# Two layers of a hybrid backbone: a recurrence's ScalarE steps are merged over two parts, emitted in smaller pieces behind the attention's exponentials, and the values' projection moves to other memory

## The chip, the cores and the metric

One core of one Trainium2 chip. The metric is the device time of one execution in microseconds; the median of three runs of the kernel before is 3753.56 us (3748.58 to 3754.28). Engines: TensorE (PE; its weight loads PEld), VectorE (DVE), ScalarE (ACT), GpSimd (POOL) and SyncE (SP), which here only issues transfers.

## The reference

Two post-norm layers over 1024 latent and 256 context tokens of width 1024, all in float32. Layer 0 mixes with an 8-head attention and, beside it, an S5 recurrence; layer 1 with a gated linear recurrence; each layer ends with a convolutional feed-forward part. The change concerns layer 0's mixer:

```python
q_l, k_l, v_l = _mla_qkv(cq_l, ckv_l, kr_l, q_norm, w_uq, kv_norm, w_ukv, rope)
att_l = _blocked_attend(q_l, k_all, v_all)          # softmax(q k^T * scale) v, 8 heads
ys_c, fin_c = _s5_bidirectional(us_c, disc, c_re, c_im, None, need_ctx)
ys_l, _ = _s5_bidirectional(us_l, disc, c_re, c_im, fin_c, True)   # complex diagonal scan
z = jax.nn.gelu(y + d_g * us); out = z * jax.nn.sigmoid(z @ w_glu)
y_lat = jnp.concatenate([att_l, out], -1) @ w_out
```

The recurrence's state is complex: each state has a real and an imaginary part, and a step multiplies it by a complex number that is constant per state, s += a * s_before, that is (re, im) += (ar*re - ai*im, ai*re + ar*im).

## The kernel before

`body` runs setup, the first modulation, loading of x, `s5_setup` (the recurrence's matrices), `in_proj` (the combined input projection), `attention`, `mix_out0` (gate and output projection) and then the feed-forward parts and layer 1, which the change does not edit. float32 matrices are split in a high part that TensorE reads in one pass and a low remainder (`split`: ScalarE copies the high part, VectorE or GpSimd subtracts), and a product is three matmuls (`mm3`, lines 103 to 105).

`attention` first projects the values of all heads (`pv`, pool `vp`), scales them on ScalarE (`vo`) and stores them in DRAM (`vd`). Then it interleaves generators; each `yield` ends a step, and `merge` takes from the generator with most of its steps left. `qk(h)` loads head h's weights, projects keys (`pk`) and queries (`pq`), finds the largest score of a row (`pS` at line 797, reduced on VectorE) and puts it in row 96 of `QT`. `attend(h)` takes 22 tiles of 128 keys: scores `pS`, exponential `p` on ScalarE, its split `ph`/`pl`, and three matmuls into `po`; three block results go out as `ao`. `A1` brings the modulation of later stages (`pada`, 80 steps with 512 KB each). `S5Half.run` is the recurrence (`S`), in two halves of 16 groups: `pV` (input matmuls, evicted into `H`), two levels of an up-sweep, 38 sequential steps on GpSimd, two levels of a down-sweep, then `pY` (output matmuls), the gelu `z`, and a store to `Zd`, which `mix_out0` loads again as `z`.

A level (`bulk`) multiplies a part of `H` by a constant per partition and state on ScalarE into `bt` (one activation per state q, part in, part out) and adds it to `H` on VectorE (direction 0) or GpSimd (direction 1). PSUM has eight banks, given by letters in `BANKS`: in the attention A has two for scores, B one for `po`, C three for `qk`, D one for the recurrence, E one for the modulation. `behind(k, inst)` keeps what is issued within it behind `inst`; `k.pace` is the last score matmul. A scheduler of the framework then sets each engine's order: emission gives the priority, buffers and readiness by its own estimates the rest; on the chip each engine, and SyncE's queue of transfers, goes strictly in that order. Pools are stacks at the left or right end of the memory, and a tile waits for what was in its place. Before, `vp` lies on the left, where the pool `W` of `qk` follows it; the exponentials' pool `PP` is on the right.

Of the kernel before, what the change touches and what calls it, by code (L numbers as in the profile page):

```python
# [17 lines left out]
D = 1024  # L18
# [28 lines left out]
def constants():  # L47

    ident = np.eye(128, dtype=np.float32)
    d16 = (np.arange(128)[:, None] % 16 == np.arange(16)[None, :]).astype(np.float32)  # L50
    pos = np.arange(SEQ)
    inv = (10000.0 ** (-np.arange(8, dtype=np.float32) / np.float32(8))).astype(np.float32)
    ar = (pos // 64).astype(np.float32)[:, None] * inv
    ac = (pos % 64).astype(np.float32)[:, None] * inv
    ang = np.concatenate([ar, ar, ac, ac], -1).T
    rope = np.zeros((64, T), np.float32)
    rope[:32, :SEQ] = np.cos(ang)
    rope[32:, :SEQ] = np.sin(ang)
    rope[:32, SEQ:] = 1.0
    s = np.arange(128)  # L60
    masks = np.zeros((128, 7, 128), np.int32)
    for l in range(7):
        h = 1 << l
        masks[:, l] = ((s[:, None] // (2 * h) == s[None] // (2 * h)) & (s[:, None] // h != s[None] // h))
    return {"k_ident": ident, "k_d16": d16, "k_rope": rope, "k_mask": masks.reshape(128, 896),
            "k_sel": np.repeat(np.eye(8, dtype=np.float32), 64, 1)}
# [152 lines left out]
def lower_bounds(k, A, S):  # L219
# [18 lines left out]
    k.mask = k.const([128, 7, 128], mybir.dt.uint8, tag="mask")  # L238

# [367 lines left out]
def in_proj(k, A, wp, places):  # L607
# [67 lines left out]
    for i in range(0, 896, 448):  # L675
        m32 = sp([128, 448], I32, tag="sq", bufs=2)
        nc.sync.dma_start(out=m32[:], in_=A["k_mask"][:, i:i + 448])
        nc.gpsimd.tensor_copy(k.mask[:].rearrange("p l t -> p (l t)")[:, i:i + 448], m32[:])
# [15 lines left out]
def attention(k, A):  # L694
# [22 lines left out]
    vp = Pool(k, "vp")  # L717
# [96 lines left out]
    def attend(h):  # L814
        b = h % 2
        q, kk_, v = QT[b], KT[b], Vt[b]
        for s, e in BLK:
# [3 lines left out]
            for i, t in enumerate(tiles):  # L821
# [3 lines left out]
                nc.scalar.activation(p[:, :n], ps[:, :n], AF.Exp, scale=SCALE)  # L825
# [20 lines left out]
    for _ in zip_longest(qk(0), some(8, A1)):  # L846
        pass
    for h in range(8):
        merge((24, attend(h)), *([(20, qk(h + 1))] if h < 7 else []), *([(34, some(34, S)), (12, some(12, A1))]))
# [10 lines left out]
class S5Half:  # L860
# [11 lines left out]
    def run(self):  # L872
        k, nc, P = self.k, self.k.nc, self.P
        E = nc.gpsimd
        for hh in range(2):
# [10 lines left out]
            for p in range(8):  # L886
# [11 lines left out]
                yield 1  # L898
# [3 lines left out]
            def bulk(i, up, d):  # L902
# [5 lines left out]
                src, dst = ((h, 2 * h), (h, 0))[d] if up else ((0, h), (2 * h, h))[d]  # L908
                for q0 in range(0, 8, m):
# [3 lines left out]
                    for b in range(2):  # L913
                        for a in range(2):
                            for q in range(m):
                                nc.scalar.activation(t[b][:, a, q], raw(H, 16 * 161 * d + (8 * b + q0 + q) * 161 + src, [[2 * h, n]]),  # L916
                                                     AF.Copy, scale=Mh[:, i, d, a, b, q0 + q:q0 + q + 1])
                        o = raw(H, 16 * 161 * d + q0 * 161 + dst, [[8 * 161, 2], [161, m], [2 * h, n]])
                        if b == 0:
                            yield 1  # L920
                    for b in range(2):
                        e.tensor_tensor(o, o, t[b], op=OP.add)
                    yield 1

            def both(levels, up):

                g = [chain(*(bulk(i, up, d) for i in levels)) for d in range(2)]
                for x in zip_longest(*g):
                    yield 1
# [7 lines left out]
            for (pf, cf, df), (pb, cb) in zip(seq, seb):  # L937
# [7 lines left out]
                yield 1  # L945
            yield from both((1, 0), False)
            for p in range(8):
# [8 lines left out]
                for q in range(2):  # L956
# [8 lines left out]
                    nc.scalar.activation(t[:, q], ps[:, :160], AF.Square, scale=0.5)  # L965

# [7 lines left out]
                yield 1  # L974
# [571 lines left out]
def body(tc, A, out, stop=None, taps=None):  # L1546
    nc = tc.nc
    k = Ctx()
    k.tc, k.nc, k.pace = tc, nc, None
# [128 lines left out]
```

## Time and profile before

| | |
|---|---|
| median of 3 runs | 3753.56 us |
| profiled execution | 3752.72 us |
| its span | 3750.9 us |
| mean granted TensorE clock | 0.967 of 2.4 GHz |
| TensorE busy | 3562.0 us, 95% |
| VectorE, ScalarE, GpSimd busy | 54%, 32%, 29% |
| first to last exponential | 333.5 to 903.5 us |

An average over 3.75 ms says little on one stage: ScalarE's 32% are up to 19 of 20 us in some stretches of the attention. Matmuls are pipelined, and a recorded one is longer than the time to the next one's start, so a busy TensorE may still have small gaps.

### The profile page before, as it was taken

How to read it: one execution, taken by the hardware profiler on the slowest of the kernel's cores; microseconds unless marked ns; L12 is line 12 of the kernel's file. 1: busy time of each engine (PE TensorE's matmuls, PEld its weight loads, DVE VectorE, ACT ScalarE, POOL GpSimd, SP SyncE). 2: the span in 40 equal slices, each digit the busy share in tenths (PEclk: the TensorE clock that was granted, in tenths of full speed). 3: DMA queues.
4: the chain of work that ended last, by engine and by line, in shares of the span. 5: the costliest groups of instructions: out<-in, count | busy, mean ns of one | idle time of the engine just before them, and what ended most of it. 6: DMA issues, size and time to landing. Idle time of an engine off the chain costs nothing.

```text
span 3750.9 us, 47623 instructions
## 1 busy us (share of the span) xinstructions
PE 3562.0 (95%) x19001; PEld 2899.7 (77%) x19001; DVE 2008.3 (54%) x3201; ACT 1210.6 (32%) x2312; POOL 1086.1 (29%) x1041
## 2 busy tenths in 40 slices
PE   6987899889999999999998999999999999999997
PEld 3764565556788888888887889898987888888885
DVE  7735654556464444444447555565664744444445
ACT  2236756666342111111124322222231411212123
POOL 3626523723351111111124311211122622222122
PEclk8997999889999999999999999999999999999998
DMA  7463354314111111111110210111122111111111
GB/s 246 120 163 98 95 139 139 99 38 147 53 33 42 40 38 36 34 40 34 34 46 29 74 34 29 34 32 37 32 67 89 51 40 51 51 40 55 41 46 45
DMA packets 294303, 243.06 MB, mean 65 GB/s; under 512 B 41214, under 2 KB 255576, under 8 KB 293056
## 3 DMA queue, kind: packets, MB, share of 16 engines
q1 hardware_dynamic: 289152, 227.32, 20.4%
q10 hardware_dynamic: 4928, 12.69, 1.0%
q8 instruction: 149, 2.44, 0.3%
q14 instruction: 74, 0.61, 0.1%
HBM read 203.79 MB, written 38.28 MB: 65 GB/s over the span
## 4 chain that ended last, share of the span: by engine, by line
PE 82%; ACT 4%; DVE 3%; POOL 3%; DMA 2%; issue 1%; SPq 0%; ACTq 0%; POOLq 0%; DVEq 0%
PE pa L105 5%; PE pa L103 5%; PE pa L104 5%; PE po L103 5%; PE pg L103 5%; PE pg L105 5%; PE pg L104 5%; PE po L104 5%; PE po L105 5%; PE ph L104 3%; PE ph L105 3%; PE ph L103 3%; PE pA L1429 3%; ACT bt L916 3%; PE pmix L103 2%; PE pmix L104 2%
## 5 line engine op out<-in xcount | busy, mean ns | idle before, releaser
L114 POOL TENSOR_TENSOR w<-ws,w 128x1024 fp32r<-128x1024 f32 (+1 forms) x205 | 499.9, 2443 | 1575.0 <-ACT w L111 1464.8
L1061 DVE SCALAR_TENSOR_TENSOR acc<-po,mod,acc 128x512 f32<-128x512 f32 (+1 forms) x456 | 309.4, 679 | 557.2 <-PE po L105 556.9
L103 PE MATMUL po<-hh,w 128*128 128x512 f32 (+1 forms) x912 | 341.6, 375 | 11.0 <-DVE acc L1061 9.2
L111 ACT ACTIVATE w<-ws 128x1024 fp32r<-128x1024 f32 (+1 forms) x207 | 216.9, 1049 | 408.7 <-PE pg L105 165.4
L104 PE MATMUL po<-hl,w 128*128 128x512 f32 (+1 forms) x912 | 335.4, 368 | 5.9 <-DVE hl L114 5.8
L105 PE MATMUL po<-hh,w 128*128 128x512 f32 (+1 forms) x912 | 334.8, 367 | 0.0
L103 PE MATMUL pa<-uh,w 128*128 128x512 f32 (+1 forms) x896 | 331.6, 370 | 0.9 <-ACT w L111 0.8
L104 PE MATMUL pa<-ul,w 128*128 128x512 f32 (+1 forms) x896 | 330.1, 369 | 0.1
L105 PE MATMUL pa<-uh,w 128*128 128x512 f32 (+1 forms) x896 | 326.4, 370 | 0.8 <-POOL w L114 0.8
L103 PE MATMUL pg<-uh,w 128*128 128x512 f32 (+1 forms) x872 | 324.2, 372 | 1.9 <-ACT w L111 1.9
L104 PE MATMUL pg<-ul,w 128*128 128x512 f32 (+1 forms) x872 | 322.6, 370 | 0.0
L105 PE MATMUL pg<-uh,w 128*128 128x512 f32 (+1 forms) x872 | 321.5, 372 | 0.6 <-POOL w L114 0.6
L103 PE MATMUL ph<-uh,w 128*128 128x512 f32 (+1 forms) x624 | 239.8, 385 | 1.2 <-ACT uh L1047 1.2
L104 PE MATMUL ph<-ul,w 128*128 128x512 f32 (+1 forms) x624 | 235.6, 378 | 0.8 <-DVE ul L1049 0.8
L105 PE MATMUL ph<-uh,w 128*128 128x512 f32 (+1 forms) x624 | 235.5, 377 | 0.0
L103 PEld LDWEIGHTS po<-hh,w 128*128 128x128 f32 x912 | 172.9, 190 | 46.1 <-DVE acc L1061 12.0
L104 PEld LDWEIGHTS po<-hl,w 128*128 128x128 f32 x912 | 173.6, 190 | 37.9 <-DVE hl L114 7.0
L1114 ACT ACTIVATE a<-pa 128x512 f32<-128x512 f32 (+1 forms) x112 | 61.3, 547 | 431.6 <-PE pa L105 430.5
L105 PEld LDWEIGHTS po<-hh,w 128*128 128x128 f32 x912 | 173.5, 190 | 30.2
L103 PEld LDWEIGHTS pa<-uh,w 128*128 128x128 f32 x896 | 168.7, 188 | 32.7 <-ACT w L111 1.0
L105 PEld LDWEIGHTS pa<-uh,w 128*128 128x128 f32 x896 | 168.6, 188 | 32.2 <-POOL w L114 1.3
L104 PEld LDWEIGHTS pa<-ul,w 128*128 128x128 f32 x896 | 168.6, 188 | 32.2 <-DVE ul L1049 0.3
(401 smaller groups left out, 7948.3 us busy)
## 6 DMA issues: line engine op xcount, KB each, us to landing
ws<-in_ffn_w_in_dram SPq DMA_DIRECT2D x88, 512.0 KB
adaw<-in_ada_w_dram SPq DMA_DIRECT2D x80, 512.0 KB
ws<-in_ffn_w_out_dram SPq DMA_DIRECT2D x44, 512.0 KB
ws<-in_hg_w_in_dram SPq DMA_DIRECT2D x40, 512.0 KB
w<-in_ada_w_dram SPq DMA_DIRECT2D x8, 1024.0 KB
ws<-in_ev_w_out_dram SPq DMA_DIRECT2D x10, 512.0 KB
ws<-in_hg_w_out_dram SPq DMA_DIRECT2D x10, 512.0 KB
ws<-in_ev_w_in_dram SPq DMA_DIRECT2D x9, 512.0 KB
```

Of the source, the lines that this page charges most:

```text
L103: nc.tensor.matmul(ps, lhsT=w[0], rhs=x[0], start=start, stop=False)
L104: nc.tensor.matmul(ps, lhsT=w[0], rhs=x[1], start=False, stop=False)
L105: return nc.tensor.matmul(ps, lhsT=w[1], rhs=x[0], start=False, stop=stop)
L111: nc.scalar.activation(hi, src, AF.Copy)
L114: (nc.gpsimd if elo == "p" else nc.vector).tensor_tensor(lo, src, hi.bitcast(F), op=OP.subtract)
L916: nc.scalar.activation(t[b][:, a, q], raw(H, 16 * 161 * d + (8 * b + q0 + q) * 161 + src, [[2 * h, n]]), AF.Copy, scale=Mh[:, i, d, a, b, ...
L1061: k.nc.vector.scalar_tensor_tensor(a, ps[:, :e - s], modcol(k, layer, seg, 1 if s >= SEQ else 0, ct), a, op0=OP.mult, op1=OP.add)
L1114: nc.scalar.activation(at[t][:, col(o):col(o) + e - o], ps[:, o - s:e - s], AF.Copy)
L1429: nc.tensor.matmul(ps[:, i * 128:i * 128 + 128], lhsT=km[:, c:c + 128], rhs=raw(Q, c, [[2 * hs, 64 // hs], [SEQ + hs, 2], [1, hs]]), start ...
```

## The change

- `bulk`: one activation per state and factor takes both parts of the input at once (`at(0, q0 + q, src, [[8 * 161, 2]])`): t[0] is the real factor times (re, im), t[1] the imaginary factor times (re, im). The addition is one over both parts for t[0], and for t[1] a subtraction and an addition of half the size with the parts crossed. The activations stand behind the last exponential emitted (`k.exp`), and a step ends after every second q. `both` gives a step to each direction in turn.
- `run` has more and smaller steps: one per direction of `pV`, one per two sequential steps, one per q of `pY` and of its stores.
- `attention`: `qk(0)` is emitted together with eight modulation steps and 32 of the recurrence's; each head then takes 23 instead of 34. In head 7, without a `qk` beside it, A has three banks and D three.
- `vp` is allocated on the right, where the exponentials' pool follows it.
- The mask of layer 1 comes from the host as uint8 and is loaded once in the setup on ScalarE's queue, instead of two int32 loads and casts on GpSimd in `in_proj`.

```diff
@@ in_proj @@
-    for i in range(0, 896, 448):
-        m32 = sp([128, 448], I32, tag="sq", bufs=2)
-        nc.sync.dma_start(out=m32[:], in_=A["k_mask"][:, i:i + 448])
-        nc.gpsimd.tensor_copy(k.mask[:].rearrange("p l t -> p (l t)")[:, i:i + 448], m32[:])
@@ attention @@
-    vp = Pool(k, "vp")
+    vp = Pool(k, "vp", "right")
...
-                nc.scalar.activation(p[:, :n], ps[:, :n], AF.Exp, scale=SCALE)
+                k.exp = nc.scalar.activation(p[:, :n], ps[:, :n], AF.Exp, scale=SCALE)
...
-    for _ in zip_longest(qk(0), some(8, A1)):
-        pass
+    merge((20, qk(0)), (8, some(8, A1)), (32, some(32, S)))
     for h in range(8):
-        merge((24, attend(h)), *([(20, qk(h + 1))] if h < 7 else []), *([(34, some(34, S)), (12, some(12, A1))]))
+        if h == 7:
+            k.banks = dict(k.banks, A="013", D="645")
+        merge((24, attend(h)), *([(20, qk(h + 1))] if h < 7 else []), *([(23, some(23, S)), (12, some(12, A1))]))
@@ S5Half.run, bulk @@
-                    for b in range(2):
-                        for a in range(2):
-                            for q in range(m):
-                                nc.scalar.activation(t[b][:, a, q], raw(H, 16 * 161 * d + (8 * b + q0 + q) * 161 + src, [[2 * h, n]]),
-                                                     AF.Copy, scale=Mh[:, i, d, a, b, q0 + q:q0 + q + 1])
...
-                    for b in range(2):
-                        e.tensor_tensor(o, o, t[b], op=OP.add)
-                    yield 1
+                    for q in range(m):
+                        with behind(k, k.exp):
+                            for b in range(2):
+                                nc.scalar.activation(t[b][:, :, q], at(0, q0 + q, src, [[8 * 161, 2]]), AF.Copy,
+                                                     scale=Mh[:, i, d, b, 0, q0 + q:q0 + q + 1])
+                        if q % 2:
+                            yield 1
+                    o = at(0, q0, dst, [[8 * 161, 2], [161, m]])
+                    e.tensor_tensor(o, o, t[0], op=OP.add)
+                    for a, op in ((0, OP.subtract), (1, OP.add)):
+                        o = at(a, q0, dst, [[161, m]])
+                        e.tensor_tensor(o, o, t[1][:, 1 - a], op=op)
```

SyncE's queue at the end of `in_proj`, before (`ws` of w_ukv are the values' weights, `adaw` modulation weights, `U` and `RO` the recurrence's inputs):

```order
L677 DMA sq<-in_k_mask_dram 128x448 x2
L721 DMA ws<-in_mla_w_ukv_dram 128x8x64 x2
L627 DMA Sd<-sTt 128x1280
L254 DMA adaw_2331<-in_ada_w_dram 128x1024
L254 DMA adaw_2348<-in_ada_w_dram 128x1024
L878 DMA U<-Sd 16x16x160 x8
```

The same place now (`wqs`, `wks` are the weights of `qk`):

```order
L742 DMA wqs<-in_mla_w_uq_dram 128x3x32
L743 DMA wqs<-in_mla_w_uq_dram 128x3x64
L749 DMA wks<-in_mla_w_ukv_dram 128x2x64
L628 DMA Sd<-sTt 128x1280
L255 DMA adaw_2326<-in_ada_w_dram 128x1024
L876 DMA U<-Sd 16x16x160 x8
L886 DMA RO<-s5R 128x4x128 x2
L255 DMA adaw_2397<-in_ada_w_dram 128x1024
L742 DMA wqs<-in_mla_w_uq_dram 128x3x32
L743 DMA wqs<-in_mla_w_uq_dram 128x3x64
L749 DMA wks<-in_mla_w_ukv_dram 128x2x64
L255 DMA adaw_2471<-in_ada_w_dram 128x1024
```

Head 0's weights stand where the mask and the values' weights stood; the latter follow two rows further on, behind the third modulation load.

ScalarE's queue in a down-sweep, before, in head 1:

```order
L825 ACTIVATE p<-pS 128x512
L916 ACTIVATE bt_3980<-H,Mh 128x40 x8
L111 ACTIVATE ph<-p 128x512
L811 ACTIVATE QT_2160<-pm 1x256
L916 ACTIVATE bt_3980<-H,Mh 128x40 x2
L111 ACTIVATE KT_2154<-tq 64x512
L111 ACTIVATE ph<-p 128x512
L837 ACTIVATE ao<-po 65x512
L825 ACTIVATE p<-pS 128x512
L916 ACTIVATE bt_3980<-H,Mh 128x40 x3
L916 ACTIVATE bt_4076<-H,Mh 128x80 x6
L825 ACTIVATE p<-pS 128x512
```

The same sweep now, at the end of head 1 (its start):

```order
L822 ACTIVATE p<-pS 128x512
L111 ACTIVATE ph<-p 128x512
L808 ACTIVATE QT_2153<-pm 1x512
L822 ACTIVATE p<-pS 128x256
L915 ACTIVATE bt_3482<-H,Mh 128x2x40
L915 ACTIVATE bt_3483<-H,Mh 128x2x40
L915 ACTIVATE bt_3482<-H,Mh 128x2x40
L915 ACTIVATE bt_3483<-H,Mh 128x2x40
L915 ACTIVATE bt_3513<-H,Mh 128x2x40
L915 ACTIVATE bt_3514<-H,Mh 128x2x40
```

Activations that stood in groups of 1 to 16 between exponentials and splits stand here as one run of 32 between an exponential and its split `ph`; it goes on like the last rows.

SyncE's queue at the end of the attention, before:

```order
L972 DMA Zd<-z 8x16x160 x2
L317 DMA ws<-in_s_w_glu_dram 128x4x256
L1195 DMA z<-Zd 128x1280 x4
L1197 DMA sel<-in_k_sel_dram 8x512
L317 DMA ws<-in_ev_w_out_dram 128x8x128 x2
L838 DMA attd<-ao 64x512
L839 DMA atts<-ao 1x512
```

The same place now:

```order
L978 DMA Zd<-z 8x16x160 x6
L835 DMA attd<-ao 64x512
L836 DMA atts<-ao 1x512
L1201 DMA z<-Zd 128x1280 x3
L835 DMA attd<-ao 64x256
L836 DMA atts<-ao 1x256
L1201 DMA z<-Zd 128x1280
L1203 DMA sel<-in_k_sel_dram 8x512
```

The loads of the recurrence's output stood ahead of two large `ao` stores of head 7, and stand now behind both, one of the four behind the small one too.

## Rows read from the trace of the kernel before

**Rows 1.** Page: span, busy us of the engines, busy tenths of TensorE in 40 slices.

```profile
span 3750.9 us, 47623 instructions
...
PE 3562.0 (95%) x19001; PEld 2899.7 (77%) x19001; DVE 2008.3 (54%) x3201; ACT 1210.6 (32%) x2312; POOL 1086.1 (29%) x1041
...
PE   6987899889999999999998999999999999999997
```

**Rows 2.** Windows: length, busy PE, PEld, DVE, ACT, POOL, granted clock, DMA share, GB/s.

```profile
225.00:333.50 108.50, 77.55 (x437) 52.02 (x435) 48.08 (x75) 59.05 (x174) 32.97 (x44) 0.80 0.59 147
333.50:398.60 65.10, 60.94 (x308) 38.76 (x308) 34.13 (x53) 32.86 (x61) 50.88 (x120) 0.91 0.33 98
398.60:472.10 73.50, 67.50 (x328) 42.73 (x327) 52.22 (x85) 62.86 (x191) 34.15 (x44) 0.91 0.33 99
623.10:703.60 80.50, 64.12 (x352) 40.39 (x352) 40.94 (x65) 57.85 (x162) 51.47 (x80) 0.85 0.33 100
703.60:794.10 90.50, 71.12 (x341) 45.11 (x340) 49.08 (x76) 65.52 (x192) 49.35 (x81) 0.81 0.25 73
858.00:909.10 51.10, 46.84 (x207) 33.70 (x205) 26.96 (x33) 39.08 (x68) 17.02 (x13) 0.96 0.40 123
640.00:680.00 40.00, 23.62 (x109) 14.10 (x109) 18.02 (x24) 34.57 (x116) 23.05 (x27) 0.70 0.22 66
740.00:780.00 40.00, 20.62 (x74) 12.82 (x72) 18.47 (x23) 37.73 (x138) 14.12 (x11) 0.65 0.15 45
```

**Rows 3.** Lines by form, 200 to 930 us: busy, mean ns, idle before.

```profile
L825 ACT ACTIVATE p<-pS 128x512 f32<-128x512 f32 x160 | 94.2, 592 | 77.7 <-PE pS L105 61.6 <-DVE pl L114 4.4 <-POOL pl L114 3.9
L111 ACT ACTIVATE ph<-p 128x512 fp32r<-128x512 f32 x160 | 98.3, 627 | 14.7 <-PE po L831 12.5
L916 ACT ACTIVATE bt<-H,Mh 128x80 f32<-128x80 f32 x256 | 69.5, 354 | 1.9 <-DVE H L922 1.5
L916 ACT ACTIVATE bt<-H,Mh 128x40 f32<-128x40 f32 x256 | 67.3, 354 | 1.7 <-POOL H L944 1.6
L896 ACT ACTIVATE H<-pV 128x320 f32<-128x320 f32 x32 | 13.9, 433 | 18.5 <-PE pV L893 17.7 <-ACT vo L731 0.4
L922 POOL TENSOR_TENSOR H<-H,bt 128x640 f32<-128x640 f32 x24 | 40.9, 1703 | 66.2 <-ACT bt L916 64.4 <-ACT H L896 1.4
```

**Rows 4.** Chain that ended last, 240 to 340 us: start, length, what.

```profile
243.54 10.21 DMA U<-Sd
253.81 6.79 DMA adaw<-in_ada_w_dram
...
280.92 6.27 DMA vd<-vo
...
310.44 15.65 ACT bt L916 x61
...
333.54 0.60 ACT p L825
```

**Rows 5.** By tile: values' projection and modulation copies, first and last start.

```profile
L105 PEld LDWEIGHTS pv<-w,late x20: 187/188/331, 252.4 to 282.5; 128*128 128x128 f32 x20
L262 DVE COPY adam<-pada x10: 408/424/426, 280.9 to 790.6; 128x256 f32<-128x256 f32 x10
```

**Rows 6.** SyncE's queue at the end of the attention: start, length, issue.

```profile
869.09 2.46 SPq L1195 DMA_DIRECT2D z<-Zd  x4
...
906.83 0.42 SPq L839 DMA_DIRECT2D atts<-ao  x1
```

**Rows 7.** ScalarE in the same stretch: start, length, operation.

```profile
874.78 1.17 ACT L1215 ACTIVATE zs<-z 128x512 fp32r<-128x512 f32 x1
...
887.08 1.28 ACT L1232 ACT_TABLE_LOAD   x1
...
905.69 0.59 ACT L837 ACTIVATE ao<-po 65x512 f32<-65x512 f32 x1 [1.05 <-PE po L832]
```

**Rows 8.** TensorE there: start, length, and what it waited for.

```profile
909.13 0.79 PE L103 MATMUL pglu<-zs,w 128*128 128x512 f32 x1 [1.83 <-ACT ao L837]
```

More of the change, by code (lines that the diff above doesn't have):

```diff
@@ L60, in constants @@
     s = np.arange(128)
-    masks = np.zeros((128, 7, 128), np.int32)
+    masks = np.zeros((128, 7, 128), np.uint8)
     for l in range(7):
@@ L238, in lower_bounds @@
     k.mask = k.const([128, 7, 128], mybir.dt.uint8, tag="mask")
+    nc.scalar.dma_start(out=k.mask[:], in_=A["k_mask"].rearrange("p (l t) -> p l t", l=7))
 def ada(*args):
@@ L908, in bulk @@
                 src, dst = ((h, 2 * h), (h, 0))[d] if up else ((0, h), (2 * h, h))[d]
+                at = lambda part, q, s0, dims: raw(H, 16 * 161 * d + (8 * part + q) * 161 + s0, dims + [[2 * h, n]])
                 for q0 in range(0, 8, m):
@@ L912, in bulk @@
                          .rearrange("p (a q x) -> p a q x", a=2, q=m) for b in range(2)]
-                    for b in range(2):
-                        for a in range(2):
-                            for q in range(m):
-                                nc.scalar.activation(t[b][:, a, q], raw(H, 16 * 161 * d + (8 * b + q0 + q) * 161 + src, [[2 * h, n]]),
-                                                     AF.Copy, scale=Mh[:, i, d, a, b, q0 + q:q0 + q + 1])
-                        o = raw(H, 16 * 161 * d + q0 * 161 + dst, [[8 * 161, 2], [161, m], [2 * h, n]])
-                        if b == 0:
-                            yield 1
-                    for b in range(2):
-                        e.tensor_tensor(o, o, t[b], op=OP.add)
-                    yield 1
+                    for q in range(m):
[4 more added lines that the diff above has]
+                        if q % 2:
+                            yield 1
+                    o = at(0, q0, dst, [[8 * 161, 2], [161, m]])
[3 more added lines that the diff above has]
+                        e.tensor_tensor(o, o, t[1][:, 1 - a], op=op)
             def both(levels, up):
                 g = [chain(*(bulk(i, up, d) for i in levels)) for d in range(2)]
-                for x in zip_longest(*g):
-                    yield 1
+                while g:
+                    for x in list(g):
+                        if next(x, None) is None:
+                            g.remove(x)
+                        else:
+                            yield 1
             nc.vector.memset(H[:, 1, :, :, 160], 0.0)
@@ L936, in run @@
             assert len(seq) == len(seb)
-            for (pf, cf, df), (pb, cb) in zip(seq, seb):
+            for x, ((pf, cf, df), (pb, cb)) in enumerate(zip(seq, seb)):
                 sl = lambda f, b, dims: raw(H, f, [[b - f + 16 * 161, 2]] + dims)
@@ L944, in run @@
                 E.tensor_tensor(sl(df, cb, [[161, 16]]), t2[:], sl(cf, cb, [[161, 16]]), op=OP.add)
-                yield 1
+                if x % 2:
+                    yield 1
             yield from both((1, 0), False)
@@ L965, in run @@
                     nc.scalar.activation(t[:, q], ps[:, :160], AF.Square, scale=0.5)
+                    yield 1
                 nc.vector.scalar_tensor_tensor(t[:], t[:], 1.0 / (4.0 * 0.044715), z[:], op0=OP.add, op1=OP.mult)
@@ L973, in run @@
                                                   ap=[[160, 8], [1280, 16], [1, 160]]), in_=z[:, q])
-                yield 1
+                    yield 1
 def coefs(k, layer, ln, nxt):
@@ L1548, in body @@
     k = Ctx()
-    k.tc, k.nc, k.pace = tc, nc, None
+    k.tc, k.nc, k.pace, k.exp = tc, nc, None, None
     k.banks, k.turn, k.out = BANKS, {}, None
```

## The prediction

> **What bounds the kernel now.** The page first: TensorE is busy 3562.0 of 3750.9 us, and of the 40 slices of 94 us its tenths fall below 9 in six of the first nine, in the 21st and in the last [rows 1]. So among what the change edits the attention with the recurrence, the 3rd to 10th slice, is open. Windows come second, cut at the first exponential of each head (the 1st, 23rd, ... of 176). Before head 0 lie 108.5 us in which TensorE works 77.6 at a clock of 0.80. Head 0, with no recurrence activations, takes 65.1 us; heads 1, 4 and 5, which hold 128, 96 and 128 of them, take 73.5, 80.5 and 90.5 [rows 2]. In the two worst stretches ScalarE is busy 34.6 and 37.7 of 40 us, TensorE only 23.6 and 20.6, and the granted clock falls to 0.70 and 0.65, a mix of 2.4 and 1.2 GHz [rows 2]. Third, the lines name ScalarE's load: 512 `bt` activations, 69.5 + 67.3 us, or 0.267 us each start to start, as dear for 40 elements as for 80 [rows 3]. Fourth, the chain: 61 of them run as one piece of 15.65 us ahead of the first exponential, which starts at 333.54 [rows 4]. Elsewhere no engine's busy time fills a head; there the exponentials' pace (0.592 + 0.627 us each on ScalarE [rows 3], two PSUM banks) sets it.
>
> The profiled execution took 3752.72 us, 1.8 more than its span; the median of the runs is 3753.56. The sum is made against 3752.7.
>
> **A, the first exponential comes earlier.** Before, values' projection, the recurrence's input and eight modulation steps go first, and end at 282.5 and 280.9 [rows 5]; head 0's keys and queries follow, and the 96 activations that stand in front of the first exponential. Now head 0's weights head SyncE's queue, its projections stand on TensorE among that same work, and only 16 of the new activations come before the first exponential. What still has to be over by then are the eight modulation steps, paced by their transfers (10.21 us for U, then 6.79 for the first weights [rows 4]). I add to 282 the keys, queries and scores of head 0 that now share this stretch: some 50 matmuls at 3562.0/19001 = 0.19 us [rows 1], 10 us, and 4 us (my choice between 0 and the 6.79 that the first modulation weights took) for the values' weights, which now queue behind a third modulation load that waits until TensorE has used the first. First exponential at 296: 37 us earlier. TensorE then needs the values themselves: a store of them took 6.27 us [rows 4]; as long again for the way back puts them 12 to 13 us behind the projection's end, which in this order is near 290, so at 303, and the first product waits for them while six score tiles are already made. That takes 4 back. Four of the sixteen input groups of the recurrence's first half, 16 matmuls x 0.19 us, move behind the first exponential: 3. A = -30. Bounds: -42 (start at 290, no wait) and -8 (the projection drags to 310 and the values with it).
>
> **B, fewer and smaller steps on ScalarE.** 512 activations become 256 of twice the elements. The trace has no 160-element one from SBUF; it lies between the 80-element form, 69.5/256 = 0.271 us, and the 320-element eviction, 13.9/32 = 0.434 [rows 3]; on the line between them 0.325. Half of the 256 have 80 elements. In the heads now stand 240 (128 of 80, 112 of 160): 128 x 0.271 + 112 x 0.325 = 71 us (64 to 83 with the ends). Before, 352 in heads 1, 4 and 5 were 352 x 0.267 = 94 us, and these heads were 8.4 + 15.4 + 25.4 = 49 us longer than head 0 [rows 2]: 0.52 us lost for each. The order shows that the new ones are not all in small steps: one run of 32 stands between an exponential and its split at the end of head 1 and one in head 6, others of 24 in heads 0 and 4, 112 in all (30 us); the remaining 128 (41 us) come in twos to eights with exponentials between. I charge the runs 0.65 and the rest 0.2: 20 + 8 = 28. B = 28 - 49 = -21. Ends: nothing lost, -49; everything lost, +22.
>
> The row has 40 and 80 elements at the same 354 ns, start to start 0.26 and 0.27 [rows 3]. The Trainium skill (ScalarE: Activation LUTs, *What ACT_TABLE_LOAD costs*) says that an activation with one pointer operand takes about 280 ns plus 0.833 ns per element and overlaps the next by 93. That speaks for the merging less than the row does: 313 and 347 ns alone, 40 cheaper than 80, which this trace does not bear out. By the rule, as an estimate, the new ones would be 0.25 and 0.32 us, 68 us for the 240, and B the same within 1 us.
>
> The additions on VectorE and GpSimd go from two of 640 elements to one of 640 and two of 320 per half: 12 more instructions on either engine, on GpSimd at most 12 x 1.7 = 20 us [rows 3] over seven heads, on an engine that is busy 50.9 of 65.1 us in head 0 and 34.2 of 73.5 in head 1 [rows 2]; cover: the exponentials' pace. Without the cover the recurrence's chain is late, 20 at most; below nothing excluded, since no element is saved. I take 0. The mask's two loads and two casts (late in the projections, on SyncE and GpSimd) go, and one small load stands in the setup: 0, within 3 either way, as the early order shifts a little.
>
> **C, the end of the attention.** Before, the recurrence is done by the start of head 7: its outputs come back from 869.09 on, the first is used at 874.78, 5.7 us after the issue, and half of the gate's first block (24 of 48 matmuls, with two table loads of 1.28 us to go to the sigmoid and back) hides under head 7 [rows 6, 7]. Now outputs are still made in head 7; three of the four loads stand on SyncE behind the stores of the last large `ao`, the fourth behind those of the small one, and the gate's 48 matmuls behind all of head 7. Before, TensorE is on the gate again 2.9 us after that `ao` (909.13 against 905.69 + 0.59) [rows 7, 8]. Now: 1.0 for the two stores (906.28 to 907.25 [rows 6]), the issues to about 4, 5.7 to land, and 1.17 twice for the split's two parts: 12, so 9 later, and 24 matmuls x 0.19 = 4.6 us still to do. Head 7 gives back some 4 of its 51.1 [rows 2], two table loads and a split that ScalarE no longer carries there. C = +10; bounds 0 and +20.
>
> Sum: 3752.7 - 30 - 21 + 10 = 3711.7, so **3712 us**, 1.1% below the median.
>
> **Rivals.** (1) No early start: values and transfers hold head 0, A = -8. For it: the transfers of 240 to 282 stay the same and the values' weights are later in the queue. Against: 96 activations do leave that place. Time 3752.7 - 8 - 21 + 10 = 3734. (2) The runs hide: B = -45, since scores run ahead and the runs are shorter: 32 x 0.271 = 9 us against 15.65 [rows 4]. Against: `ph` has three buffers, and 9 us are four tiles at head 7's 51.1/22 = 2.3 us [rows 2]. Time 3752.7 - 30 - 45 + 10 = 3688. (3) Slower: at an end of head 1, 4 and 6 and in head 0 ScalarE's queue holds a run in front of `ph`, TensorE is in order behind the `po` that needs it, and all 71 us show; the clock falls at each of the four runs as in the two stretches at 0.70 and 0.65 [rows 2], where 12 to 14 us at half speed lost 6 to 7, 5 apiece for the shorter runs: B = 71 + 20 - 49 = +42, time 3752.7 - 30 + 42 + 10 = 3775. It decides once more than 60 of the 71 us are exposed. For it: those two stretches, where ScalarE was the only full engine. Against: 0.52 was the mean of much longer runs. (4) The order holds only on paper: the recurrence falls behind, `pY` blocks TensorE in heads 2, 6 and 7, and the gains of A and B cancel with C at +20: about 3750.
>
> **How the numbers follow.** Forecast 0.52, its own range 3692 to 3733; rival 1 0.18; rival 2 0.13; rival 3 0.10; rival 4 0.07. A measurement here can tell 0.2%, 7.5 us. Faster, below 3746: 0.52 + 0.13 and most of rival 1, 0.15: 0.80. Same: the rest of rival 1, most of 4: 0.09. Slower: 0.11. The range that leaves out a part of rivals 2, 3 and 4 is 3686 to 3748.
>
> **What would show it.** A: first exponential near 296 (290 to 325), and no piece of `bt` over 3 us before it. B: `bt` near 0.27 and 0.33 us start to start, 256 of them; heads 1, 4 and 5 near 65 to 72 us, ScalarE full nowhere for 20 us, the clock at 2.4 GHz but for short dips at the four runs. C: a gap on TensorE of 8 us or more before the gate's matmuls, where before it was 1.83 [rows 8]. Wrong, if heads are above 75 us each, if the first product waits past 315, or if TensorE's idle time before `pY` passes 10 us.

## The result, and the profile after

The changed kernel takes 3708.29 us (median of 4 runs, 3707.79 to 3714.1) against 3751.99 for the kernel before (4 runs, 3748.58 to 3754.28). The ratio is 0.9894, 95% interval [0.9881, 0.9906]; the quotient of the two medians is 0.9884. The forecast was 3712. The profiled execution took 3707.79 us, and its page begins so; against [rows 1] the span is 44.9 us shorter and ScalarE 48.5 us less busy, and two of TensorE's tenths in the attention, the 4th and the 8th, rise to 9.

```profile
span 3706.0 us, 47407 instructions
...
PE 3550.4 (96%) x19001; PEld 2898.0 (78%) x19001; DVE 2014.3 (54%) x3213; ACT 1162.1 (31%) x2054; POOL 1101.6 (30%) x1051
...
PE   6989899989999999999998999999999999999997
```

The windows of the changed kernel, with the columns of [rows 2]: heads 0 to 2, 4, 6 and 7, and the two worst stretches of 20 us.

```profile
301.70:366.80 65.10, 62.17 (x339) 38.53 (x342) 45.03 (x68) 48.80 (x111) 44.87 (x63) 0.95 0.47 130
366.80:430.70 63.90, 54.64 (x317) 35.45 (x311) 34.13 (x59) 42.46 (x91) 50.01 (x106) 0.94 0.41 122
430.70:510.20 79.50, 77.71 (x399) 52.30 (x402) 51.70 (x83) 47.76 (x114) 29.21 (x31) 0.89 0.39 112
586.50:658.70 72.20, 69.54 (x427) 43.30 (x426) 45.69 (x74) 53.55 (x127) 28.56 (x28) 1.00 0.45 134
713.80:788.20 74.40, 60.85 (x258) 44.90 (x257) 48.23 (x68) 53.77 (x132) 40.20 (x54) 0.82 0.05 14
788.20:852.00 63.80, 58.22 (x282) 44.01 (x280) 29.08 (x42) 38.33 (x85) 18.51 (x13) 0.95 0.34 94
420.00:440.00 20.00, 9.97 (x39) 5.80 (x37) 12.28 (x16) 17.15 (x52) 5.53 (x5) 0.59 0.21 64
740.00:760.00 20.00, 9.35 (x23) 5.96 (x23) 15.84 (x17) 18.09 (x51) 9.64 (x6) 0.53 0.00 1
```

Head 0 starts 31.8 us earlier and is as long as before; the stretches in which ScalarE is full and the clock falls are still there, half as long. The 256 new activations, by form, answer to [rows 3]: 88.9 us of busy time instead of 136.8 (divided by the count, this is what the prediction calls start to start), and both forms are dearer than a one-part one of 80 elements had been.

```profile
L915 ACT ACTIVATE bt<-H,Mh 128x160 f32<-128x160 f32 x128 | 46.2, 436 | 5.7 <-DVE H L923 4.7 <-DVE H L920 0.5
L915 ACT ACTIVATE bt<-H,Mh 128x80 f32<-128x80 f32 x128 | 42.7, 431 | 4.3 <-POOL H L948 4.3
```

Where they still form a run, ScalarE's timeline shows it (start, length, operation, and the idle time before it with what ended that):

```profile
418.75 10.52 ACT L915 ACTIVATE bt<-H,Mh 128x80 f32<-128x80 f32 x32 [0.98 <-POOL H L948]
429.18 0.62 ACT L111 ACTIVATE QT<-tq 96x512 fp32r<-96x512 f32 x1
429.70 0.58 ACT L834 ACTIVATE ao<-po 65x512 f32<-65x512 f32 x1
430.17 0.41 ACT L111 ACTIVATE ph<-p 128x256 fp32r<-128x256 f32 x1
```

A run of 10.5 us starts as soon as GpSimd's last serial step is done, and behind it stand the next head's queries' split (QT), an `ao` and an exponential's split. The first of these is what TensorE then waits for. Its longest waits between 200 and 920 us (total, times, longest):

```profile
PE pS L794 <- ACT QT L111: 9.7, 2, 7.6
PE pk L103 <- ACT QT L808: 8.2, 1, 8.2
```

The end of the attention on SyncE, ScalarE and TensorE answers to [rows 6 to 8]. The recurrence's last outputs go out in head 7 (six stores that take the queue to 848); three of its loads stand behind the large `ao`'s stores, the fourth behind the small one's; `zs` waits 2.19 us for the first, and TensorE 5.10 us for `zs`.

```profile
831.29 16.83 SPq L978 DMA_DIRECT2D Zd<-z  x6
849.24 0.48 SPq L835 DMA_DIRECT2D attd<-ao  x1
849.77 0.42 SPq L836 DMA_DIRECT2D atts<-ao  x1
850.29 1.32 SPq L1201 DMA_DIRECT2D z<-Zd  x3
...
853.08 0.32 SPq L1201 DMA_DIRECT2D z<-Zd  x1
```

```profile
854.22 1.06 ACT L1221 ACTIVATE zs<-z 128x512 fp32r<-128x512 f32 x1 [2.19 <-DMA z<-Zd]
```

```profile
849.96 0.28 PE L829 MATMUL po<-pl,V 128*128 128x256 f32 x1
855.34 1.22 PE L103 MATMUL pglu<-zs,w 128*128 128x512 f32 x2 [5.10 <-ACT zs L1221]
```

To compare kernels I cut each trace at the same four events: end of the input projections, first exponential, end of the last `ao`, start of the gate's last matmul. These three windows hold the whole difference: what lies behind them is 2797.0 us before and 2797.6 after, what lies ahead 237.4 and 233.3. Of the changed kernel:

```profile
233.30:301.70 68.40, 56.59 (x330) 36.27 (x329) 36.07 (x59) 28.30 (x54) 20.54 (x34) 0.88 0.79 197
301.70:852.00 550.30, 508.88 (x2715) 343.38 (x2714) 328.20 (x521) 358.63 (x805) 281.36 (x411) 0.93 0.38 106
852.00:908.40 56.40, 52.47 (x205) 37.06 (x206) 47.76 (x44) 29.18 (x44) 17.68 (x10) 0.91 0.50 177
```

The same windows of all kernels, in us, where "idle" is TensorE's in the heads (length less busy), and the ratio is to the kernel before, timed on the same chip, where its median was 3750.2 to 3752.6 us. One of the four runs of e10_seqdve fell in a slow state (5545.94 us at a clock of 0.578) and is left out of its median.

| kernel | start | heads | gate | sum | ScalarE busy in heads | idle | median | ratio |
|---|---|---|---|---|---|---|---|---|
| before | 96.1 | 575.6 | 44.8 | 716.5 | 383.3 | 53.0 | 3751.99 | |
| changed | 68.4 | 550.3 | 56.4 | 675.1 | 358.6 | 41.4 | 3708.29 | 0.9894 [0.9881, 0.9906] |
| b1_merged | 95.4 | 535.2 | 44.9 | 675.5 | 345.8 | 31.8 | 3709.53 | 0.9896 [0.9882, 0.9911] |
| b2_vp_right | 71.1 | 587.0 | 51.7 | 709.8 | 404.9 | 79.0 | 3746.22 | 0.9990 [0.9982, 0.9999] |
| e1_vp_left | 88.2 | 545.9 | 47.9 | 682.0 | 345.2 | 29.3 | 3718.27 | 0.9907 [0.9894, 0.9921] |
| e2_unmerged | 69.4 | 590.5 | 50.7 | 710.6 | 403.6 | 80.8 | 3746.56 | 0.9987 [0.9978, 0.9996] |
| e6_banks | 68.3 | 544.3 | 63.9 | 676.5 | 358.1 | 38.7 | 3709.43 | 0.9896 [0.9880, 0.9913] |
| e9_flat | 68.2 | 550.7 | 50.9 | 669.8 | 351.6 | 40.6 | 3703.22 | 0.9872 [0.9857, 0.9887] |
| e10_seqdve | 69.2 | 571.1 | 44.8 | 685.1 | 362.8 | 46.3 | 3712.46 | 0.9897 [0.9882, 0.9912] |
| e11_paced | 70.0 | 533.4 | 112.2 | 715.6 | 350.2 | 35.0 | 3739.80 | 0.9972 [0.9961, 0.9984] |
| e12_qv | 66.5 | 551.6 | 60.9 | 679.0 | 349.7 | 42.2 | 3709.28 | 0.9891 [0.9877, 0.9905] |
| e13_half | 67.8 | 535.6 | 58.5 | 661.9 | 319.2 | 30.7 | 3694.51 | 0.9857 [0.9844, 0.9869] |
| e14a_sttv | 66.4 | 551.3 | 44.9 | 662.6 | 329.3 | 36.9 | 3696.84 | 0.9864 [0.9851, 0.9877] |
| b3_sttv | 92.6 | 559.2 | 46.0 | 697.8 | 321.0 | 33.4 | 3730.56 | 0.9950 [0.9936, 0.9965] |

### The profile page after: what moved, and what is told of

Read it like the earlier page. It is cut to its first block, busy times and chain, and to the rows that moved or that the text cites. A ratio compares the mean times of both kernels' runs of the same rounds, so it can differ in the third digit from the quotient of the medians.

```text
span 3706.0 us, 47407 instructions
## 1 busy us (share of the span) xinstructions
PE 3550.4 (96%) x19001; PEld 2898.0 (78%) x19001; DVE 2014.3 (54%) x3213; ACT 1162.1 (31%) x2054; POOL 1101.6 (30%) x1051
## 4 chain that ended last, share of the span: by engine, by line
PE 85%; DVE 3%; POOL 3%; ACT 1%; DMA 1%; issue 1%; SPq 0%; ACTq 0%; POOLq 0%; DVEq 0%
PE pa L105 5%; PE pa L103 5%; PE pa L104 5%; PE pg L103 5%; PE po L103 5%; PE pg L105 5%; PE pg L104 5%; PE po L104 5%; PE po L105 5%; PE ph L104 4%; PE ph L105 4%; PE ph L103 4%; PE pA L1435 3%; PE pmix L103 2%; PE pmix L104 2%; PE pmix L105 2%
## 5 line engine op out<-in xcount | busy, mean ns | idle before, releaser
L105 PEld LDWEIGHTS pa<-uh,w 128*128 128x128 f32 x896 | 168.7, 188 | 32.2 <-POOL w L114 1.3
L104 PEld LDWEIGHTS pa<-ul,w 128*128 128x128 f32 x896 | 168.6, 188 | 32.2 <-DVE ul L1055 0.4
```

The source lines that it names most:

```text
L104: nc.tensor.matmul(ps, lhsT=w[0], rhs=x[1], start=False, stop=False)
L105: return nc.tensor.matmul(ps, lhsT=w[1], rhs=x[0], start=False, stop=stop)
```

## The experiments

### Which part of the change carries the gain

**e1_vp_left**, the early start taken back:

```
-    vp = Pool(k, "vp", "right")
+    vp = Pool(k, "vp")
```

> The changed kernel with the pool of the values' projection back on the left, as before the change; all else stays. Theory (step A is its own gain): 64 of the merged activations stand ahead of the first exponential again, which starts at 325 to 333 us instead of 301.7; the recurrence's outputs are further along by head 7, so the gap before the gate is under 2 us instead of 5 (step C gone, some -8). Time 3708 + 27 - 8 = about 3727 (3718 to 3738). Rival (the early start is given back later, because ScalarE and the recurrence's chain set the heads): first exponential late as above, but the end within 5 us of 3708.

The start is late again (first exponential at 322.3) and the tail short, but the median is only 10 us above the changed kernel's, at the lower edge of the theory's range, and the two intervals overlap. In the profiled executions 19.8 us of start buy 6.9 in the three windows (10.9 in the span): about half of the early start or more is given back.

**e2_unmerged**, the merged activation split again:

```
-    nc.scalar.activation(t[b][:, :, q], at(0, q0 + q, src, [[8 * 161, 2]]), AF.Copy, ...)
+    for a in range(2):
+        nc.scalar.activation(t[b][:, a, q], at(a, q0 + q, src, []), AF.Copy, ...)
```

> The changed kernel with each merged activation split in two again (512 of one part each, emitted at the same places). Theory (step B is the number of ScalarE instructions): the bt group goes from 88.9 us back to about 137 us of start-to-start time, 48 more, of which a half shows as in the kernel before: 3708 + 24 = 3732 (3722 to 3745), the heads that hold the runs 7 to 10 us longer each. Rival 1 (the gain of B is the smaller steps and the places, not the merging): within 5 us of 3708. Rival 2 (runs are exposed in full): 3750 or more.

Nearly all of the gain is gone: 38 us more by the medians (35 by the ratios), above the theory's range and just below rival 2. ScalarE is 45.0 us busier in the heads and these are 40.2 longer. One wait of TensorE holds that, 9.7 us in the changed kernel:

```profile
PE pS L794 <- ACT QT L111: 56.5, 6, 15.5
```

Its cause is on ScalarE: small steps in the program do not keep the 64 activations apart, they come as one run, and the queries' split behind it.

```profile
433.44 16.37 ACT L916 ACTIVATE bt<-H,Mh 128x40 f32<-128x40 f32 x64 [2.12 <-POOL H L949]
...
450.44 0.63 ACT L111 ACTIVATE QT<-tq 96x512 fp32r<-96x512 f32 x1
```

**b1_merged**, the kernel before with the merging alone:

```
-    for a in range(2):
-        for q in range(m):
-            nc.scalar.activation(t[b][:, a, q], raw(H, ...), AF.Copy, scale=Mh[:, i, d, a, b, ...])
+    for q in range(m):
+        nc.scalar.activation(t[b][:, :, q], at(0, q0 + q, src, [[8 * 161, 2]]), AF.Copy, ...)
...
-    for b in range(2):
-        e.tensor_tensor(o, o, t[b], op=OP.add)
+    (one addition of both parts, then one subtraction and one addition of a part each)
```

> The kernel before with the merged activations and their three additions alone: order of emission, place of the values' projection, banks and mask as before. Theory, after the run that split them again (3746.6): merging carries nearly all of the gain, because a run of bt on ScalarE holds the queries' split and with it the maxima's matmuls on TensorE. Then the wait of pS on QT falls from 22.0 us to 12 or less, heads 1, 4 and 5 shrink by 8 to 14 us each, the first exponential comes 3 to 8 us earlier, no new gap before the gate: 3752 - 35 = 3717 (3710 to 3725). Rival (merging pays only with the small steps and the early start): 3735 to 3748.

It is as fast as the whole change, and below the range that I had given. Its heads:

```profile
330.70:865.90 535.20, 503.40 (x2708) 337.42 (x2706) 323.83 (x524) 345.83 (x759) 267.90 (x394) 0.97 0.38 110
```

Start and gate are those of before; the heads give 40.4 us: 21.2 of TensorE's idle time and 19.2 of its busy time, which shrinks for as many matmuls (2705 and 2708) while the granted clock of the stretch goes from 0.92 to 0.97. The wait on the queries' split, which I had named as the cause, falls less than I had expected, from 22.0 to 17.5 us between 200 and 920 us (12 or less was the theory). TensorE's longest waits in the heads of the kernel before:

```profile
PE pS L797 <- ACT QT L111: 15.5, 3, 14.6
PE pY L960 <- DVE H L922: 10.7, 3, 6.6
PE po L830 <- ACT ph L111: 6.3, 1, 6.3
```

In those of b1_merged:

```profile
PE pS L797 <- ACT QT L111: 12.3, 2, 10.5
...
PE po L830 <- ACT ph L111: 1.2, 2, 0.6
```

The wait that shrinks most is that of the recurrence's outputs (`pY`) on VectorE's addition to `H`, which stands behind `bt`: 10.5 us of it go, down to 0.2, then 5.1 of the wait on `ph` and 3.2 of that on the queries' split. So a long run of `bt` holds TensorE in three ways, and in this order of emission the queries' split is the smallest of the three parts that merging frees. ScalarE's timeline in head 5 of the kernel before:

```profile
741.31 16.43 ACT L916 ACTIVATE bt<-H,Mh 128x40 f32<-128x40 f32 x64 [1.25 <-POOL H L944]
757.76 0.58 ACT L811 ACTIVATE QT<-pm 1x512 fp32r<-1x512 f32 x1
758.37 0.63 ACT L111 ACTIVATE ph<-p 128x512 fp32r<-128x512 f32 x1
758.91 1.06 ACT L825 ACTIVATE p<-pS 128x512 f32<-128x512 f32 x2
759.86 16.50 ACT L916 ACTIVATE bt<-H,Mh 128x80 f32<-128x80 f32 x64
```

The same place of b1_merged, in the old order of emission:

```profile
709.37 10.53 ACT L916 ACTIVATE bt<-H,Mh 128x80 f32<-128x80 f32 x32 [2.13 <-POOL H L946]
719.80 0.40 ACT L111 ACTIVATE KT<-tq 64x256 fp32r<-64x256 f32 x1
720.10 0.62 ACT L111 ACTIVATE QT<-tq 96x512 fp32r<-96x512 f32 x1
...
721.10 1.06 ACT L825 ACTIVATE p<-pS 128x512 f32<-128x512 f32 x2
722.05 2.76 ACT L916 ACTIVATE bt<-H,Mh 128x160 f32<-128x160 f32 x8
724.71 0.63 ACT L111 ACTIVATE ph<-p 128x512 fp32r<-128x512 f32 x1
```

The first run is a third shorter. The second, of 64 before, comes in eights of 2.8 us with exponentials and splits between them.

**b2_vp_right**, the kernel before with the early start alone (the one line of e1_vp_left, the other way round):

> The kernel before with the pool of the values' projection on the right, and nothing else. Theory (the early start is mostly given back later): first exponential 20 to 30 us earlier, at 303 to 313, but the end only 3 to 12 us earlier, 3740 to 3749, since the recurrence's chain does not move with it and its activations land in heads that did not hold them. Rival (step A as predicted, a gain of its own of 30 less 10 in the tail): 3732 (3728 to 3738).

As expected: the first exponential comes 27.7 us earlier and the end, by the ratio, about 4. The heads, which now hold 96 activations more, are 11.4 us longer, and the gate 6.9.

**e6_banks**, the change without its switch of PSUM banks:

```
-        if h == 7:
-            k.banks = dict(k.banks, A="013", D="645")
```

> The changed kernel without its switch of PSUM banks in head 7 (there the scores have banks 0, 1 and 3 and the recurrence 4, 5 and 6; here two and one, as in the other heads). It closes the list of the change's parts that have not run alone. Theory (the tail waits for the recurrence's chain, and the switch only lets its outputs run through more banks): the last output comes 5 to 10 us later after head 7 begins, the gate later with it: 3708 + 4 to +10 = 3715. Rival (the exponentials' pace sets head 7 and the switch is worth nothing): 3708 within 4.

The rival holds on time, not in its reason: without the switch the heads are 6.0 us shorter and the gate is 7.5 us longer, and the time is the same. The smaller steps of emission and the mask have no run of their own; that they bring nothing follows only from the changed kernel being no faster than b1_merged, and there together with the early start.

### What a ScalarE activation costs here

**e9_flat**, as many elements in one row:

```
-    nc.scalar.activation(t[b][:, :, q], at(0, q0 + q, src, [[8 * 161, 2]]), ...)
+    nc.scalar.activation(t[b] flat [2*n*q : 2*n*q+2*n], raw(H, 16*161*d + (q0+q)*161 + 1-d, [[h, 2*n]]), ...)
```

> The changed kernel with the merged activations' input and output as one-dimensional rows of as many elements (160 or 80); they read other columns than the recurrence wants, so its values are not computed, only its work. Theory (the two-dimensional pattern is what made one activation 431 to 436 ns where 40 and 80 elements in one row had been 354): about 350 ns for the form of 80 and 400 to 420 for the form of 160, some 10 to 15 us less on ScalarE, time 3700 to 3706. Rival (the price is set by the elements or by the two parts' memory, not by the pattern): 431 and 436 stay, time 3708 within 4.

```profile
L915 ACT ACTIVATE bt<-H,Mh 128x160 f32<-128x160 f32 x128 | 44.5, 419 | 3.3 <-DVE H L924 2.5 <-DVE H L921 0.4
L915 ACT ACTIVATE bt<-H,Mh 128x80 f32<-128x80 f32 x128 | 33.5, 353 | 1.3 <-POOL H L949 1.3
```

That is 78 ns less for the form of 2 x 40 and 17 for 2 x 80, together 10.9 us of ScalarE. But the edit changes two things: it puts the elements in one row, and it halves the step between them, from 4 floats to 2 for the shorter form and from 2 to 1 for the longer (`[2 * h, n]` became `[h, 2 * n]`). Which of them it is was not shown. An estimate from the rows speaks for the step of 4: 353 and 419 ns make 0.83 ns an element, so that 40 elements would take 320 ns, and the 40 of the kernel before, also at a step of 4, took 354. If an element costs twice as much at that step, 40 of them take 353 ns and 2 x 40, with 17 for the second row, 436, near the 354 and 431 measured.

The time is as the theory has it, 3703, though the interval still meets the changed kernel's. It is not a gain of the heads, which are as long as before (550.7 us): of the 5.3 us that the windows lose, the gate has 5.5.

**e12_qv**, the queries' split off ScalarE:

```
-            split(nc, q[0][0:96, s:e], q[1][0:96, s:e], t[0:96, :n], elo="v")
+            split(nc, q[0][0:96, s:e], q[1][0:96, s:e], t[0:96, :n], ehi="v", elo="v")
```

> The changed kernel with the queries' split taken off ScalarE: its rounded half is copied by VectorE instead (24 copies of 96 x 512 or 256 elements). Theory (what makes a run of bt cost TensorE time is the queries' split queued behind it on ScalarE): TensorE's wait of pS on QT falls from 9.7 us to under 3, the time to 3708 - 5 to -10 = about 3701. Rival 1 (the exponentials' splits ph are behind the same run and take over as the wait): po on ph grows by what pS on QT loses, 3708 within 4. Rival 2 (24 copies of some 0.7 us more on VectorE hold the maxima): 3713 or more.

No gain. The wait of `pS` on ScalarE's QT is gone, that on VectorE's is 6.2 us in six pieces, `po` on GpSimd's `pl` grows from 3.6 to 6.0, and TensorE's idle time in the heads is 42.2 us after 41.4. Rival 1 has the time, but not by the wait that it named (`po` on `ph` goes from 2.7 to 3.4): the loss went to several smaller ones. Taking one victim out of the queue behind a run does not shorten the run.

**e13_half**, one of the two activations left out:

```
-                            for b in range(2):
+                            for b in range(1, 2):
...
-                    e.tensor_tensor(o, o, t[0], op=OP.add)
+                    e.tensor_tensor(o, o, t[1], op=OP.add)
```

> The changed kernel with one of the two merged activations of each step left out (128 instead of 256; the addition that used its result reads the other one's), so the recurrence's values are not computed; the additions and all else stay. It measures what ScalarE's bt work costs: 240 x 0.347 = 83 us stand in the heads now, 41 of them go. Theory, from the runs so far (the heads are 535, 550 and 590 us long with 67, 83 and 126 us of bt in them: about one us for one us): the heads 36 to 42 us shorter, time 3708 - 40 = 3668 (3662 to 3676). Rival 1 (half of it shows, the rate that the prediction took, 0.52): 3687 (3682 to 3692). Rival 2 (what is left is hidden): 3700 to 3710.

```profile
736.20 5.33 ACT L915 ACTIVATE bt<-H,Mh 128x80 f32<-128x80 f32 x16 [2.01 <-POOL H L948]
```

My theory of one for one fell, and the time, 3694.5, lies between the two rivals. ScalarE is 39.4 us less busy in the heads, and these are 14.7 us shorter: 0.37. Adding 45.0 us in e2_unmerged cost 40.2, 0.89; 37.5 less in b1_merged gave 40.4, 1.08. So there is no one rate: between longest runs of 16 to 20 us and of 10.5 us nearly all showed, between 10.5 and 5.3 us a third. Whether the length of the runs sets that or the sum of ScalarE's work, which fell with it, no run separates. Nearest comes e11_paced below, with all 256 activations in runs of 4.1 us at most: TensorE's idle time in its heads is 35.0 us, after 41.4 in the changed kernel and 30.7 here, but these heads also hold 140 matmuls less than the changed kernel's.

### The tail

**e10_seqdve**, the serial steps on VectorE:

```
-                E.tensor_tensor(t1[:]...   (and the two operations behind it)
+                nc.vector.tensor_tensor(t1[:]...
```

> The changed kernel with the recurrence's 38 serial steps of each half (3 small operations a step, 1.8 us a step in the trace) on VectorE instead of GpSimd; all else stays. Theory (step C comes from the recurrence's chain ending inside head 7): the serial stretches shrink from 70 us to 30 to 45, the last output of the recurrence is made 20 us or more before head 7's end, its loads are issued ahead of head 7's stores, and TensorE's wait before the gate falls from 5.1 us to under 2: 3708 - 8 to -12 = about 3698 (3692 to 3703). Rival (the serial steps hold VectorE's queue, with the maxima and splits behind them, and TensorE waits for these): the gap goes but heads 1, 2, 5 and 6 grow by as much or more: 3705 to 3725.

The rival holds on time. The serial stretches did not shrink (the first took 350.7 to 424.0 us, in the changed kernel 349.2 to 418.1): the steps' own operations fill 36.1 us of it on VectorE and filled 39.4 on GpSimd, and the rest is mostly other work of the same queue, the maxima and splits above all. But the order that came with it puts all four loads ahead of the last three pairs of stores, and the gate is back at 44.8 us. The heads are 20.8 longer with 70.1 us more of VectorE, and the time is not better.

**e11_paced**, emitted later and finer:

```
-    merge((20, qk(0)), (8, some(8, A1)), (32, some(32, S)))
+    merge((20, qk(0)), (8, some(8, A1)), (16, some(16, S)))
...
-                if x % 2:
-                    yield 1
+                yield 1
```

> The changed kernel with the recurrence emitted later and in more steps (16 instead of 32 steps ahead of head 0, one step for each serial step instead of one for two): no run of bt between two exponentials' instructions is longer than 16 (before: twice 32), but all 16 output evictions of the second half fall into head 7 instead of 12. Theory (runs cost time in heads, lateness costs it in the tail): heads 1 to 6 together 10 to 16 us shorter, the gate's end 8 to 16 us later after head 7's end; 3708 within 6. Rival 1 (the runs cost nothing): heads as they were, 3716 to 3724. Rival 2 (the tail costs nothing more): 3692 to 3698.

The runs are gone and the heads 16.9 us shorter, but they also hold 140 matmuls less: the second half's outputs run alone behind head 7, and the gate ends 55.8 us later in that kernel's last window, at a granted clock of 0.70. The time is 3739.8 us where 3708 was expected: the term for lateness that I had put at 8 to 16 us was far too small.

### A faster version

**e14a_sttv**, half of the activations turned into a fused multiply and add on VectorE:

```
+    nc.scalar.activation(t[1][:, :, q], at(0, q0 + q, src, [[8 * 161, 2]]), AF.Copy, scale=Mh[:, i, d, 1, 0, ...])
+    o = at(0, q0 + q, dst, [[8 * 161, 2]])
+    nc.vector.scalar_tensor_tensor(o, at(0, q0 + q, src, [[8 * 161, 2]]), Mh[:, i, d, 0, 0, ...], o,
+                                   op0=OP.mult, op1=OP.add)
-    e.tensor_tensor(o, o, t[0], op=OP.add)
```

> The changed kernel with the real half of each step as one fused multiply and add on VectorE (128 of them, 160 or 80 elements) in place of 128 activations on ScalarE and 24 additions of 640 elements on VectorE and GpSimd; the result is the same sum. ScalarE loses 44 us, VectorE gains 128 x 0.35 to 0.45 less 15 = 30 to 43, GpSimd loses 21; the recurrence's loads come ahead of head 7's last stores. Theory (ScalarE's bt work is what shows, VectorE has room: 328 of 550 us busy in the heads): 3708 - 25 to -40 = about 3676 (3666 to 3686). Rival (VectorE becomes what TensorE waits for, as with the serial steps on VectorE, whose heads were 21 us longer for 70 us of VectorE): 3695 to 3715.

It beats both kernels: its interval ends below the changed kernel's. But at 3697 us it is in the rival's range and not in the theory's, and the reason that I gave does not hold. Its heads and its gate:

```profile
301.00:852.30 551.30, 514.37 (x2743) 345.79 (x2742) 360.37 (x631) 329.27 (x692) 265.10 (x398) 0.95 0.39 110
852.30:897.20 44.90, 42.59 (x183) 30.14 (x184) 38.89 (x42) 23.80 (x40) 17.54 (x11) 1.00 0.51 166
```

The heads are as long as the changed kernel's, with 29.4 us less on ScalarE and 32.2 more on VectorE. The gain of 11.2 us in the span is the gate's 11.5: the recurrence's last output is made at 813.6 instead of 843.3 us and its loads go out ahead of head 7's stores.

```profile
820.97 1.22 SPq L978 DMA_DIRECT2D Zd<-z  x2
822.30 2.29 SPq L1201 DMA_DIRECT2D z<-Zd  x4
...
848.93 0.49 SPq L835 DMA_DIRECT2D attd<-ao  x1
```

**b3_sttv**, the same edit on b1_merged:

> The kernel before with the merged activations and the same fused multiply and add on VectorE, in the old order of emission and without the early start. Theory (what ScalarE loses shows in either order, and the early start and the small steps come to nothing): 3709.5 - 20 to -35, within 8 us of the same edit on the changed kernel. Rival (with less on ScalarE the early start pays): 10 us or more above that one.

The theory fell and the rival's time holds: 21 us slower than b1_merged, and 34 above e14a_sttv, of which the start has 26.2. TensorE's idle time in the heads is about as in b1_merged (33.4 and 31.8 us), its busy time 22.4 us longer for as many matmuls, at a granted clock of 0.94 instead of 0.97. Which of the new places of VectorE's work does that is open; no run tells it apart.

## Why the prediction was right, and where it was not

**The sum** held, in part by luck: 41 us less forecast, 44.9 found between the two profiled executions, and each term has about its size in the windows. A: 27.7 earlier at the start (forecast 30; the first exponential at 301.7 for 296, the first product at 309.7 for 303); another 4.1 came ahead of it, of which the kernels with the old mask show 2.1 and 2.7 as well (235.3 and 234.7), so it is mostly not the change's. B: the heads 25.3 shorter (21); heads 1, 4 and 5 are together 53.3 shorter and head 2 is 2.6 shorter, while heads 3, 6 and 7 are 30.6 longer. C: the gate 11.6 longer (10), by the forecast mechanism: the loads behind the stores, the gate behind all of head 7. Its sizes were off and made up for each other: TensorE idles 3.9 us in that stretch (the wait of 5.1 begins ahead of it) where I had the gate 9 later, is busy 7.7 us more there for the half of the first block that no longer hides (4.6), and head 7, which was to give back 4, takes 63.8 us instead of 51.1, which counts in the heads. That C is the price of the recurrence's lateness is shown from the other side: with the loads ahead, e10_seqdve and e14a_sttv have 44.8 and 44.9 us there.

**The attribution** failed, in the step "A = -30". I took the early start as a gain of its own. Alone it is worth about 4 us by the ratio (b2_vp_right). Beside the merging it is worth 5 by the ratio and 10 by the medians, with intervals that overlap (e1_vp_left), and the whole change is no faster than the merging alone (b1_merged). Against b1_merged the changed kernel's trace wins 27.0 us at the start and returns 15.1 in the heads and 11.5 in the gate. Two things come back: the first half's activations and some matmuls that stood in the stretch ahead of head 0 now stand in the heads (idle 31.8 to 41.4, busy 503.4 to 508.9), and a recurrence that does not start earlier with the heads ends later against them (in b2_vp_right its first input matmul starts at 258.1 us, before at 260.6, and its last activation at 792.3, before at 776.0). So B was not -21 but about -40 for the merging and +15 for what A moves into the heads. The early start can pay: with the fused operation e14a_sttv, which has it, is 34 us below b3_sttv, which has not, and gives none of it back. But the emission differs between these two as well, and e10_seqdve, with as short a tail, gains nothing; what it takes for the early start to pay is open.

**The rate** of 0.52 us for a microsecond of ScalarE, from [rows 2], failed as a step. Its base was head 0, the head without activations of the recurrence, but heads 2, 6 and 7 had none either and took 82.1, 63.9 and 51.1 us. In head 2 TensorE was busy throughout:

```profile
472.10:554.20 82.10, 82.10 (x473) 56.71 (x471) 46.65 (x80) 42.52 (x98) 20.13 (x24) 1.00 0.46 132
```

So the matmuls that fall into a head set its length as well, and the sentence that elsewhere the exponentials' pace sets a head was wrong: 22 of them with their splits take ScalarE 22 x (0.592 + 0.627) = 27 us. What the runs put in the place of the rate stands under e13_half: nearly all showed down to runs of 10.5 us, a third below that. The victim was named only in part: I had the exponential's split `ph` behind the runs, but the largest waits were on the queries' split and on the recurrence's own additions, and in e2_unmerged TensorE waits 56.5 us for the queries' split and for `ph` 1.3 us in all.

**The unit prices** were low: 0.361 and 0.334 us of busy time each for 0.325 and 0.271. With one row and half the step, e9_flat has 0.348 and 0.262: for the shorter form the pattern is the miss, for the longer one mostly the line that I had drawn to the 320-element eviction. The Trainium skill (ScalarE: Activation LUTs, *What ACT_TABLE_LOAD costs*) gives 280 ns plus 0.833 an element with one pointer operand, so as an estimate 413 and 347 ns for 160 and 80. The one-row forms agree (419 and 353), those of 40 elements (354 for 313) and of two rows (436 for 413 and 431 for 347) do not.

**What it said would show it**: no piece of `bt` above 3 us before the first exponential, and no more than 10 us of idle time before `pY`, held. Heads 1 and 4 are in the range of 65 to 72 us or near it (63.9 and 72.2), head 5 is shorter (55.1), but the load moved: heads 2, 3 and 6 take 79.5, 76.3 and 74.4, the first two above the 75 that was named as a sign of being wrong. "ScalarE full nowhere for 20 us" failed (18.09 of 20 at 740), and so did the short dips, with a mean clock of 0.53 there.

**Two readings** were slips that the sum does not need. The 21st slice of the page is the 22nd. And in rival 3 a mean clock of 0.70 or 0.65 over 40 us is 24 or 28 us at the lower of the two levels, not 12 or 14.

## What to carry to other kernels

Count what an engine's queue holds at a time and who stands behind it: halving the number of instructions in a burst did here what spreading their emission did not. A stretch that starts earlier need not be a gain; ask where the work that left the gap goes, whether what runs beside it starts earlier too, and who is last at the end. When several edits come together, run each of the large terms alone: here the merging, forecast at 21 us, alone had the whole change's time, and the early start, forecast at 30, alone had 4 us.

## What the runs showed of the hardware

- An activation of 2 x 40 elements at a step of 4 floats took 431 ns, one of 40 in a row at that step 354 and one of 80 in a row at a step of 2 353; of 2 x 80 at a step of 2 it took 436, of 160 in a row at a step of 1 419. Rows and step changed together, so neither has a price of its own here.
- Operations of 64, 32 and 32 elements took in the median 277, 192 and 222 ns on VectorE (e10_seqdve) and 357, 252 and 278 on GpSimd (the changed kernel). A chain of 38 steps of these three still took 73 us on the one and 69 on the other, as about half of either stretch was not its own operations.
- A fused multiply and add on VectorE took 492 ns for 160 and 409 ns for 80 elements in e14a_sttv, 433 and 383 in b3_sttv; the activation that it replaces took 436 and 431 in the changed kernel, and the fused form also saves an addition.
